# Row transfers, GpSimd gates and elementwise sums of tiles in a two-layer attention kernel

## The chip, the cores and the metric

The kernel runs on one core of one Trainium2 chip. The metric is device time in microseconds (us), the median of several executions. A core has TensorE (PE: matmuls; PEld is its weight load), VectorE (DVE), ScalarE (ACT), GpSimd (POOL) and the queues that issue transfers (SP, and ACT's own). Each engine takes its instructions in the order of the program; engines wait for each other by semaphores.

## The reference

Two layers over 1024 latent tokens and 256 context tokens, width 1024, all in fp32. Layer 0 has two attentions side by side, 8 heads each, in groups of four heads that share keys and values; layer 1 has a convolution and a neighbourhood attention. What matters here is the softmax of layer 0:

```python
def gqa_attend(q, k, v, bias=None, sink=None):
    s = jnp.einsum("bqhgd,bkhd->bhgqk", q, k) * ATTN_SCALE
    if bias is not None:
        s = s + bias
    if sink is not None:        # windowed attention: one learned logit per head
        p = jax.nn.softmax(jnp.concatenate([s, sink_col], axis=-1), axis=-1)[..., :-1]
    else:
        p = jax.nn.softmax(s, axis=-1)
    return jnp.einsum("bhgqk,bkhd->bqhgd", p, v)

y_lat = jnp.concatenate([oa * jax.nn.silu(ag), ob * jax.nn.silu(bg)], axis=-1) @ w_out
```

The global attention (oa) sees all 1280 tokens. The windowed one (ob) sees the context and its own block of 128 tokens with one neighbour on each side, and has the sink. Each output is multiplied by a gate before the out-projection.

## The kernel before

**Precision.** An fp32 product is made of three matmuls in TensorE's fast format: each operand is split into a high part (a cast on ScalarE) and a low part (a subtraction on GpSimd or VectorE, `split`).

**Units and groups.** Layer 0's attention has four units of four heads: 2 and 3 are windowed, 0 and 1 global; they run in the order 2, 3, 0, 1. A unit has ten groups, one for each block of 128 queries (QORD: blocks 2, 3, 4, 0, 5, 6, 1, 7, 8, 9); a group's tile of queries is 512 columns wide, four heads by 128. Blocks 0 and 1 are context and have two tiles of keys. The other groups have ten in a global unit, and five (four at the edges) in a windowed one. Layer 1 has 16 groups of seven tiles.

**One tile** (`attn_gen`): two score matmuls into a bank st (L529 with QH, the high and low keys stacked; L533 with QL), in some windowed tiles a mask matmul, an exponential to pf, a split into ph and pl, and three tiles later (LOOK0) three value matmuls into a bank ov (L480 to L482). The value tile V has 64 columns of low parts, 64 of high parts and 64 of ones, so that L480 and L482 also sum the denominators into rows 64 to 127 of ov. There are two st banks, one ov bank and two mx banks.

**Group change.** `attn_prep` finds the maxima of the group after next: score estimates in a bank mx, reduced on VectorE (L645, L656, L664). For windowed groups VectorE then takes the maximum with the sink, and with ScalarE makes the sink's own term (L439 to L446). `attn_fin` transposes the result on TensorE (L457) and VectorE spreads it over four heads into rows 64 and up of QL (L458), which enter the score through the ones in KB. After the last tile a windowed group adds its sink with one more matmul (L485). VectorE then transposes, inverts and transposes back the denominators, multiplies ov by them (L693) and by the gate gt (L695).

**Filler.** `weave` lets projections (pq, pg), their tails (trk) and the modulation weights (`mod_steps`: pm, two loads of 1 MB ahead of each half) run between the steps of attention. A scheduler orders all of it on each engine by priority and by its own estimate of when operands are ready; the filler has the lower priority.

Of the kernel before, what the change touches and what calls it, by code (L numbers as in the profile page):

```python
# [10 lines left out]
F32 = mybir.dt.float32  # L11
# [7 lines left out]
P = 128  # L19
# [14 lines left out]
LOOK0, LOOK1 = 3, 3  # L34
AHEAD = 3
# [54 lines left out]
def tile_kernel(ctx: ExitStack, tc: tile.TileContext, a, out):  # L90
# [11 lines left out]
    mk, mwp, layer = [0], [None], [0]  # L102
# [112 lines left out]
    def mod_steps(pool, halves):  # L215

        def load(l, part, j):
            ws = []
            for d in (0, 4):
                w = pool.tile([P, 4, 512], F32, tag="mw", name=nm("mw"), bufs=2)  # L220
                SY.dma_start(w, mod_src(l, part, j, d, d + 4))
                ws.append(w)
            return ws

        ws = load(*halves[0])
        for n_, hf in enumerate(halves):
# [4 lines left out]
            for d, w in enumerate(ws):  # L231
                mod_part(pb, w, range(4 * d, 4 * d + 4))
# [5 lines left out]
            if n_ + 1 < len(halves):  # L238
                ws = load(*halves[n_ + 1])
# [153 lines left out]
    bd = const("k_bd", [12, 4], SC)  # L393
# [29 lines left out]
    def attn_prep(pool, g):  # L423
# [8 lines left out]
        yield from g.maxes(QH, mp)  # L432
        nr = 12 if g.sink is not None else 4
        nmt = pool.tile([P, 12], F32R, tag="nmt", name=nm("nmt"), bufs=2)
        if g.sink is None:
            VE.tensor_reduce(nmt[:, 0:4], mp[:, :, 0 : g.nmp], axis=AX.X, op=ALU.max)
        else:
            m8 = pool.tile([P, 4], F32, tag="m8", name=nm("m8"), bufs=2)
            VE.tensor_reduce(m8, mp[:, :, 0 : g.nmp], axis=AX.X, op=ALU.max)  # L439
            sk1, sk8 = g.sink  # L440
            VE.tensor_tensor(nmt[:, 0:4], m8, sk8, op=ALU.max)
            se = pool.tile([P, 4], F32, tag="se", name=nm("se"), bufs=2)
            VE.scalar_tensor_tensor(se, nmt[:, 0:4].bitcast(F32), -SCALE, sk1, op0=ALU.mult, op1=ALU.add)
            SC.activation(se, se, AF.Exp)
            VE.tensor_copy(nmt[:, 4:8], se)
            VE.tensor_tensor(nmt[:, 8:12], se, nmt[:, 4:8].bitcast(F32), op=ALU.subtract)  # L446
# [3 lines left out]
    def attn_fin(g):  # L450

        nr, nmt, QL = g.nr, g.nmt, g.QL
        for _ in range(FIN[layer[0]]):
            yield
        tr2 = bank("mx", nm("trn"))
        with tc.issue_after(sts[-1].ins) if sts else ExitStack():
            PE.transpose(tr2[0:nr, 0:P], nmt[:, 0:nr].bitcast(F32), ident)  # L457
        VE.tensor_tensor(QL[64 : 64 + nr, :].rearrange("p (h q) -> p h q", h=4),  # L458
# [4 lines left out]
    def attn_gen(pool, groups, vshare, look, nexts=None):  # L463
# [6 lines left out]
        def flush():  # L470
# [12 lines left out]
            if last:  # L483
                if g.sink is not None:
                    PE.matmul(g.ov, g.skm(), g.QL[0:76, :], start=False, stop=True)  # L485
# [17 lines left out]
        for _ in attn_fin(groups[0]):  # L503
            pass
# [1230 lines left out]
```

## Time and profile before

| | us |
|---|---|
| three runs | 1528.69, 1532.21, 1532.37 |
| median | 1532.21 |
| span of the profiled execution | 1528.5 |
| mean granted clock of TensorE | 0.976 |

Layer 0's attention lies between about 146 and 905 us of the span, the convolution between 940 and 1110, layer 1's attention from 1199 on. In the profile's rows a tile is named without its number; `pl<-pf,ph` is an instruction that writes pl and reads pf and ph; x is a count. A releaser is what ended an engine's idle time. Durations of matmuls overlap, so their pitch has to be read from start to start.

### The profile page before, as it was taken

The page shows a single profiled execution, that of the slowest core. Times are in us where ns is not written, and L with a number is a line of the kernel's source. Part 1 is how long each engine was busy: PE and PEld are TensorE (multiplying, and loading weights), DVE is VectorE, ACT ScalarE, POOL GpSimd, SP SyncE. Part 2 cuts the span into 40 slices and gives each one's busy share as a digit, 9 for nine tenths or more (in the row PEclk, how much of TensorE's full clock was granted, in tenths as well). Part 3 has the DMA queues.
Part 4 walks back from the last instruction along what each step waited for, and adds up shares of the span by engine and source line. Part 5 has one row for each costly group of instructions (what it writes and reads, how often), then busy time and mean ns, then how long its engine had stood idle before and what let it go on. Part 6 is the DMA issues. An engine that isn't in the chain of part 4 may idle for free.

```text
span 1528.5 us, 21545 instructions
## 1 busy us (share of the span) xinstructions
PE 1451.0 (95%) x7144; PEld 1167.2 (76%) x7144; DVE 1031.7 (67%) x2095; ACT 748.1 (49%) x1418; POOL 788.0 (52%) x628
## 2 busy tenths in 40 slices
PE   6999999998998999999999889999999999989996
PEld 2786877896896777886777568888887788868775
DVE  2643566589578856457676948899848666567766
ACT  3642433443435564447646665343334455455564
POOL 3360443555454766557645665665532434364665
PEclk9999999999999999999999999999999999989998
DMA  9564325422312246121202021210484677877642
GB/s 366 201 225 135 106 69 174 135 77 88 114 56 76 85 138 210 49 69 54 59 28 66 35 67 56 62 56 28 158 253 144 207 219 240 248 222 234 178 129 110
DMA packets 154167, 199.83 MB, mean 131 GB/s; under 512 B 14716, under 2 KB 95816, under 8 KB 154056
## 3 DMA queue, kind: packets, MB, share of 16 engines
q1 hardware_dynamic: 147392, 186.88, 38.9%
q10 hardware_dynamic: 6664, 11.57, 2.3%
q8 instruction: 56, 0.92, 0.3%
q14 instruction: 55, 0.45, 0.1%
HBM read 148.07 MB, written 49.02 MB: 129 GB/s over the span
## 4 chain that ended last, share of the span: by engine, by line
PE 79%; DVE 11%; issue 3%; DMA 3%; ACT 2%; POOL 1%; ACTq 0%; SPq 0%; DVEq 0%; POOLq 0%
PE p L352 6%; PE p L354 6%; PE p L353 6%; PE ov L480 5%; PE ov L482 4%; PE ov L481 4%; PE po L352 4%; PE st L533 4%; PE st L529 4%; PE po L353 4%; PE po L354 4%; PE pq L352 4%; PE pq L353 3%; PE pq L354 3%; PE pg L352 2%
## 5 line engine op out<-in xcount | busy, mean ns | idle before, releaser
L334 POOL TENSOR_TENSOR pl<-pf,ph 128x512 fp32r<-128x512 f32 (+4 forms) x321 | 394.0, 1239 | 384.9 <-ACT ph L331 337.3
L541 ACT ACTIVATE pf<-st 128x512 f32<-128x512 f32 x284 | 166.5, 597 | 203.6 <-PE st L533 165.2
L334 POOL TENSOR_TENSOR wl<-wr,wh 128x512 fp32r<-128x512 f32 (+2 forms) x131 | 169.3, 1302 | 136.5 <-ACT wh L331 124.0
L331 ACT CAST ph<-pf 128x512 fp32r<-128x512 f32 (+4 forms) x364 | 209.5, 588 | 27.1 <-PE ov L481 15.9
L352 PE MATMUL p<-hh,wh 128*128 128x512 f32 x448 | 176.0, 393 | 3.4 <-DVE spq L1233 1.3
L353 PE MATMUL p<-hl,wh 128*128 128x512 f32 x448 | 174.5, 390 | 0.0
L354 PE MATMUL p<-hh,wl 128*128 128x512 f32 x448 | 173.0, 391 | 0.0
L480 PE MATMUL ov<-ph,Vt 128*128 128x512 f32 (+4 forms) x364 | 141.0, 387 | 4.2 <-DVE y L693 2.0
L529 PE MATMUL st<-QH,KAt 128*128 128x512 f32 (+4 forms) x364 | 140.2, 386 | 3.9 <-ACT pf L541 3.1
L482 PE MATMUL ov<-pl,Vt 128*128 128x512 f32 (+4 forms) x364 | 141.1, 388 | 2.2 <-POOL pl L334 2.1
L481 PE MATMUL ov<-ph,Vt 128*64 128x512 f32 (+4 forms) x364 | 138.9, 381 | 0.0
L533 PE MATMUL st<-QL,KBt 68*128 68x512 f32 (+4 forms) x364 | 136.4, 386 | 0.9 <-issue 0.8
L1177 DVE SCALAR_TENSOR_TENSOR cps<-U,taps,cps 128x512 f32<-128x512 f32 x184 | 125.9, 748 | 0.7
L331 ACT CAST wh<-wr 128x512 fp32r<-128x512 f32 (+2 forms) x134 | 80.9, 613 | 84.1 <-PE po L353 15.9
L352 PEld LDWEIGHTS p<-hh,wh 128*128 128x128 f32 x448 | 84.2, 188 | 21.5 <-ACT spq L1231 1.6
L656 DVE TENSOR_REDUCE mp<-mx 128x1 f32<-128x512 f32 x128 | 85.3, 681 | 19.3 <-PE mx L655 18.3
L354 PEld LDWEIGHTS p<-hh,wl 128*128 128x128 f32 x448 | 84.1, 188 | 17.4
L353 PEld LDWEIGHTS p<-hl,wh 128*128 128x128 f32 x448 | 84.2, 188 | 17.1 <-issue 0.2
L1020 DVE SCALAR_TENSOR_TENSOR x<-po,modT,x 128x512 f32<-128x512 f32 (+1 forms) x72 | 46.9, 657 | 64.0 <-PE po L354 63.5
L352 PE MATMUL pq<-wh,hh 128*128 128x384 f32 x256 | 88.2, 344 | 1.0 <-ACT hh L331 1.0
L353 PE MATMUL pq<-wl,hh 128*128 128x384 f32 x256 | 87.3, 341 | 0.0
L354 PE MATMUL pq<-wh,hl 128*128 128x384 f32 x256 | 86.6, 342 | 0.0
(287 smaller groups left out, 3417.2 us busy)
## 6 DMA issues: line engine op xcount, KB each, us to landing
mw<-in_mod_w_dram SPq DMA_DIRECT2D x16, 1024.0 KB, 5.3
Q<-qs SPq DMA_DIRECT2D x40, 256.0 KB, 2.1
QH<-Q SPq DMA_DIRECT2D x80, 128.0 KB, 2.7
mw<-in_mod_w_dram SPq DMA_DIRECT2D x16, 512.0 KB, 6.8
wr<-in_od_d_dram SPq DMA_DIRECT2D x32, 256.0 KB, 3.1
wr<-in_ev_qkv_dram SPq DMA_DIRECT2D x16, 384.0 KB, 5.0
KAt<-KD SPq DMA_DIRECT2D x16, 384.0 KB, 6.5
wr<-in_od_wo_dram SPq DMA_DIRECT2D x22, 256.0 KB, 3.4
```

The lines of the kernel that those rows point to most:

```text
L331: acts.append(SC.copy(hi, src))
L334: (GP if leng == "g" else VE).tensor_tensor(lo, src, hi.bitcast(F32), op=ALU.subtract)
L352: PE.matmul(o, lh, rh, start=first, stop=False)
L353: PE.matmul(o, lh, rl, start=False, stop=False)
L354: last.append(PE.matmul(o, ll, rh, start=False, stop=end))
L480: PE.matmul(o, V[:, 64:192], ph[:, :n], start=(t == 0), stop=False)
L481: PE.matmul(g.ov[0:64, q0 : q0 + n], V[:, 0:64], ph[:, :n], start=False, stop=False)
L482: PE.matmul(o, V[:, 64:192], pl[:, :n], start=False, stop=(last and g.sink is None))
L529: sts.append(PE.matmul(st[:, :n], KA[:, cs], g.QH[:, q0 : q0 + n], start=True, stop=False))
L533: PE.matmul(st[:, :n], KB[0:68, cs], g.QL[0:68, q0 : q0 + n], start=False, stop=True)
L541: acts.append(SC.activation(pf[:, :n], st[:, :n], AF.Exp, scale=1.0 if g.bias else SCALE))
L1177: VE.scalar_tensor_tensor(pc, uc, w, pc, op0=ALU.mult, op1=ALU.add)
```

## The change

1. **Maxima by transfer.** KB has one row of -1 in place of four of ones. `attn_fin` copies the transposed maxima (4 rows, or 12 with the sink) to SBUF on ScalarE, and a transfer on ScalarE's queue lays them out as one row (or three) of QL. The broadcast on VectorE is gone, in both layers.
2. **Gate on GpSimd.** In layer 0 the inverse denominators are multiplied by the gate on GpSimd before they meet ov. The factor 0.5 goes into V's ones, now 2.
3. **Sink elsewhere.** The sink's logit is copied by ScalarE into the maxima before they are reduced; its term is made in `attn_fin` by GpSimd and ScalarE.
4. **Sums over tiles.** In units 2 and 3, for blocks 2 and up, the exponentials of all tiles are added up elementwise in a tile acc: three of the four additions on GpSimd, the last (every fourth) on VectorE. ADV and UADD set this. A value tile then takes two matmuls in place of three. At the end acc is split, and two matmuls with ones and the sink's one make the denominators in a bank dn; ov's halves are added after a copy on ScalarE.
5. **Buffers.** The modulation weights come in loads of 512 KB with three buffers in place of 1 MB with two: a half's fourth load takes the buffer of its first. The squares at the end of layer 0 have fewer buffers of their own.

The core of the diff:

```diff
         def load(n):
+            l, part, j = halves[n // 4]
+            w = pool.tile([P, 2, 512], F32, tag="mw", name=nm("mw"), bufs=3)
+            SY.dma_start(w, mod_src(l, part, j, 2 * (n % 4), 2 * (n % 4) + 2))
...
-            for d, w in enumerate(ws):
-                mod_part(pb, w, range(4 * d, 4 * d + 4))
+            for d in range(4):
+                mod_part(pb, ws.pop(0), (2 * d, 2 * d + 1))
+                if 4 * n_ + d + 3 < 4 * len(halves):
+                    load(4 * n_ + d + 3)
...
-        GP.memset(KB[64:68, :].bitcast(F32), 1.0)
+        GP.memset(KB[64:65, :].bitcast(F32), -1.0)
...
+        if g.sink is not None:
+            SC.copy(mp[:, :, g.nmp], g.sink[1])
+        yield from g.maxes(QH, mp)
+        VE.tensor_reduce(nmt[:, 0:4], mp[:, :, 0 : g.nmp + (g.sink is not None)], axis=AX.X, op=ALU.max)
...
+    def attn_fin(pool, g):
+        if g.sink is not None:
+            GP.tensor_tensor(se, g.sink[1], nmt[:, 0:4].bitcast(F32), op=ALU.subtract)
+            yield
+            SC.activation(se, se, AF.Exp, scale=SCALE)
+            SC.copy(nmt[:, 4:8], se)
+            yield
+            GP.tensor_tensor(nmt[:, 8:12], se, nmt[:, 4:8].bitcast(F32), op=ALU.subtract)
...
-        VE.tensor_tensor(QL[64 : 64 + nr, :].rearrange("p (h q) -> p h q", h=4),
-                         tr2[0:nr, None, 0:P].broadcast_to([nr, 4, P]),
-                         bd[0:nr, :, None].broadcast_to([nr, 4, P]), op=ALU.mult)
+        nq = QL[96 : 96 + nr, 0:P]
+        SC.copy(nq, tr2[0:nr, 0:P])
+        (SC, SY)[QDE].dma_start(QL[64 : 64 + nr // 4, :].bitcast(F32).rearrange("j (h q) -> j h q", h=4),
+                                                          nq.bitcast(F32))
...
+            if g.adds:
+                both = [(o, V[:, 0:128], ph), (o[0:64], V[:, 64:128], pl)]
+                for x_, v_, p_ in both[::-1] if last else both:
+                    PE.matmul(x_, v_, p_[:, :n], start=(t == 0 and p_ is ph), stop=(last and p_ is ph))
...
+            if g.adds:
+                dn = bank("tr", nm("dn"))
+                for k_, x in enumerate(g.acs):
+                    PE.matmul(dn[0:64, :], ones64[0] if layer[0] else V[:, 128:192], x, start=(k_ == 0), stop=(k_ == 1 and g.sink is None))
...
+            if g.adds and t > 0:
+                a_ = g.acc[:, q0 : q0 + n]
+                (VE if (t + ADV[layer[0]]) % 4 == 0 else GP).tensor_tensor(a_, a_, pf[:, :n], op=ALU.add)
+            if g.adds and t == len(g.tiles) - 1:
+                g.acs = [pool.tile([P, 512], F32R, tag=x, name=nm("ac" + x), bufs=look + 1) for x in ("ph", "pl")]
+                split(g.acc, *g.acs, "s", "v")
...
+    def ADDS(u, qb):
+        return qb >= 2 and u in UADD
...
+            if g.adds:
+                for es, cs in half:
+                    acts.append(SC.copy(y2[es], ov[64:128, cs]))
+                for es, cs in half:
+                    VE.tensor_tensor(y2[es], ov[0:64, cs], y2[es], op=ALU.add)
...
+            GP.tensor_tensor(rb, rb, g.gt.rearrange("p a q -> p (a q)"), op=ALU.mult)
-            VE.scalar_tensor_tensor(y, y, 0.5, g.gt, op0=ALU.mult, op1=ALU.mult)
```

**TensorE at the first group change of unit 3.** Before (trn is the transpose of the maxima, mx the estimates for a later group, pq a projection):

```order
L457 MATMUL trn_2811<-ident,nmt_2767 12x128
L643 MATMUL mx_2832<-KAt_489,QH_2817 128x256 x2
L352 MATMUL pq_3728<-wh_3068,hh_174 128x384
L353 MATMUL pq_3728<-wl_3069,hh_174 128x384
L354 MATMUL pq_3728<-wh_3068,hl_175 128x384
```

Now, at the same change:

```order
L461 MATMUL trn_2897<-ident,nmt_2794 12x128
L666 MATMUL mx_2919<-KAt_488,QH_2901 128x256 x2
L188 MATMUL pm_3241<-mw_2075,csil 32x512 x2
L188 MATMUL pm_3241<-mw_2079,csil 32x512 x2
L188 MATMUL pm_3241<-mw_2083,csil 32x512 x2
L666 MATMUL mx_2925<-KAt_488,QH_2901 128x256 x2
L686 MATMUL mx_2929<-KAt_488,QH_2901 128x384
L544 MATMUL st_2995<-QL_2777,KBt_483 128x512
L544 MATMUL st_3020<-QL_2777,KBt_483 128x512
```

The score matmuls with QL stand seven rows behind the transpose, and no projection stands between them; three pieces of a modulation half do, and its fourth follows seven rows later. The projections of this place stand earlier and later in the order.

**ScalarE at the next group change of unit 3, now** (the ACTIVATE rows are exponentials of a score bank; y is the copy of ov's upper half):

```order
L334 CAST ph_3221<-pf_3223 128x512
L452 CAST nmt_2917<-se_3004 128x4
L718 COPY y_3384<-ov_3260 64x256 x2
L463 CAST QL_2902<-trn_3011 12x128
L334 CAST acph_3228<-acc_3000 128x512
L464 DMA QL_2902<-QL_2902 3x4x128
L555 ACTIVATE acc_3268<-st_3263 128x512
```

Of these rows only the first and the last kind stood on ScalarE before. The row's copy and its transfer stand behind the copies of ov, which need the last value matmul, and the transfer also behind the cast of the summed tile.

**GpSimd over the first of these groups.** Before (pl is the low part of a tile of exponentials, wl that of a weight, pc and Vt the projection's tails):

```order
L334 TENSOR_TENSOR pl_2911<-pf_2912,ph_2910 128x512
L249 TENSOR_TENSOR nr_3828<-ss_3825,mhalf 128x10
L334 TENSOR_TENSOR pl_2931<-pf_2932,ph_2930 128x512
L334 TENSOR_TENSOR pl_3048<-pf_3049,ph_3047 128x512
L334 TENSOR_TENSOR wl_4017<-wr_4015,wh_4016 128x512
L334 TENSOR_TENSOR pl_3129<-pf_3130,ph_3128 128x512
```

Now:

```order
L337 TENSOR_TENSOR pl_2999<-acc_3000,ph_2998 128x512
L337 TENSOR_TENSOR pl_3024<-pf_3025,ph_3023 128x512
L561 TENSOR_TENSOR acc_3000<-acc_3000,pf_3025 128x512
L449 TENSOR_TENSOR se_3004<-sink_160,nmt_2917 128x4
L337 TENSOR_TENSOR pl_3140<-pf_3141,ph_3139 128x512
L252 TENSOR_TENSOR nr_3357<-ss_3354,mhalf 128x10
L561 TENSOR_TENSOR acc_3000<-acc_3000,pf_3141 128x512
L252 TENSOR_TENSOR nr_3517<-ss_3514,mhalf 128x10
L337 TENSOR_TENSOR pl_3222<-pf_3223,ph_3221 128x512
L454 TENSOR_TENSOR nmt_2917<-se_3004,nmt_2917 128x4
L561 TENSOR_TENSOR acc_3000<-acc_3000,pf_3223 128x512
```

Between the splits now stand the additions into acc, two powers of the projection's norms and the sink's subtractions.

Over the whole program TensorE has 76 value matmuls fewer and 32 for denominators more; VectorE has 56 broadcasts, 40 gate products and 80 small operations of the sink fewer, and 12 additions, 16 splits and 32 halves' additions more; GpSimd has 48 additions, 40 gate products and 40 small operations more; ScalarE has 56 row copies with their transfers, 16 casts of acc, 32 copies of ov's halves and 40 small copies more.

More of the change, by code (lines that the diff above doesn't have):

```diff
@@ L215, in mod_steps, with load @@
     def mod_steps(pool, halves):
[L217 to L225, printed above, removed]
+        def load(n):
+            l, part, j = halves[n // 4]
+            w = pool.tile([P, 2, 512], F32, tag="mw", name=nm("mw"), bufs=3)
+            SY.dma_start(w, mod_src(l, part, j, 2 * (n % 4), 2 * (n % 4) + 2))
+            ws.append(w)
+        ws = []
+        for n in range(3):
+            load(n)
         for n_, hf in enumerate(halves):
@@ L390, in silu2 @@
         VE.scalar_tensor_tensor(dst, dst, 1.0, psrc, op0=ALU.add, op1=ALU.mult)
-    bd = const("k_bd", [12, 4], SC)
+    cp.tile([P, 8], F32, tag="cpad", name="cpad")
     Ks, Vs = [], []
@@ L431, in attn_prep @@
         mp = pool.tile([P, 4, 4], F32, tag="mp", name=nm("mp"), bufs=2)
-        yield from g.maxes(QH, mp)
         nr = 12 if g.sink is not None else 4
         nmt = pool.tile([P, 12], F32R, tag="nmt", name=nm("nmt"), bufs=2)
[L435 to L446, printed above, removed]
+        if g.sink is not None:
+            SC.copy(mp[:, :, g.nmp], g.sink[1])
+        yield from g.maxes(QH, mp)
+        VE.tensor_reduce(nmt[:, 0:4], mp[:, :, 0 : g.nmp + (g.sink is not None)], axis=AX.X, op=ALU.max)
         g.nmt, g.nr = nmt, nr
         yield
-    def attn_fin(g):
+    def attn_fin(pool, g):
         nr, nmt, QL = g.nr, g.nmt, g.QL
-        for _ in range(FIN[layer[0]]):
+        if g.sink is not None:
+            se = pool.tile([P, 4], F32, tag="se", name=nm("se"), bufs=2)
+            GP.tensor_tensor(se, g.sink[1], nmt[:, 0:4].bitcast(F32), op=ALU.subtract)
             yield
+            SC.activation(se, se, AF.Exp, scale=SCALE)
[3 more added lines that the diff above has]
+            yield
+        else:
+            for _ in range(FIN[layer[0]]):
+                yield
         tr2 = bank("mx", nm("trn"))
@@ L502, in attn_gen @@
                     yield
-        for _ in attn_fin(groups[0]):
+        for _ in attn_fin(kvs[-1], groups[0]):
             pass
@@ L1061, in final_proj @@
                     if c < 2:
[L1062 removed]
+                        sq = op_.tile([P, 512], F32, tag="sq1", name=nm("sq1"), bufs=2)
                     else:
@@ L1434, in finish @@
                     split(y[ds], od3[hf][ds, 0], od3[hf][ds, 1], "s", "v")
-            g = Group(no=gi, copy=lambda: copy_k(hd), load_q=load_q, load_b=load_b, maxes=maxes, nmp=2, bias=True, ahead=ahead, sink=None, tiles=tiles, den=den, finish=finish,
+            g = Group(no=gi, copy=lambda: copy_k(hd), load_q=load_q, load_b=load_b, maxes=maxes, nmp=2, bias=True, ahead=ahead, sink=None, tiles=tiles, finish=finish, adds=False,
                       start=start, gate=gate,
```

104 lines of the change are left out of this document (58 added, 46 removed).

## The prediction

> **What bounds the kernel now.** I read the page first, then the busy times of chosen stretches, TensorE's own waits, the timeline for the pitch of its matmuls, and the groups of instructions for durations.
>
> ```profile
> span 1528.5 us, 21545 instructions
> PE 1451.0 (95%) x7144; PEld 1167.2 (76%) x7144; DVE 1031.7 (67%) x2095; ACT 748.1 (49%) x1418; POOL 788.0 (52%) x628
> PE 79%; DVE 11%; issue 3%; DMA 3%; ACT 2%; POOL 1%; ACTq 0%; SPq 0%; DVEq 0%; POOLq 0%
> ```
>
> TensorE is busy for 95% of the span and makes 79% of the chain that ended last. So a change pays in two ways only: fewer passes on TensorE, or fewer of the 77.5 us in which it stands still (1528.5 - 1451.0). No other engine is near its limit over the whole span; in single stretches some are.
>
> ```profile
> core 0: us, PE busy (x) PEld busy (x) DVE busy (x) ACT busy (x) POOL busy (x), PEclk, DMA share, GB/s
> 330.00:360.00 30.00, 27.82 (x160) 23.36 (x159) 27.97 (x53) 12.67 (x28) 17.42 (x14) 1.00 0.31 98
> 360.00:380.00 20.00, 18.09 (x76) 13.80 (x76) 17.81 (x40) 10.26 (x23) 11.48 (x8) 0.85 0.24 79
> 460.00:520.00 60.00, 53.14 (x269) 42.21 (x267) 53.90 (x116) 29.75 (x64) 33.09 (x26) 0.97 0.26 81
> PE mx L655 <- DVE mp L656: 7.8, 14, 1.9
> PE trn L457 <- DVE nmt L436: 2.5, 3, 1.0
> PE trn L457 <- DVE nmt L446: 2.1, 3, 1.3
> PE ov L482 <- POOL pl L334: 2.1, 4, 1.2
> PE mx L643 <- DVE QL L458: 1.8, 3, 1.1
> ```
>
> The first stretch and the second hold the first groups of unit 3. VectorE is busy for 45.8 of 50 us there, TensorE for 45.9, and after 4.1 us of its idleness the granted clock falls to 0.85. In 460 to 520, where windowed groups give way to global ones without filler, TensorE misses 6.9 us and VectorE is busy for 53.9 of 60. The waits (total, times, longest) name VectorE 14.2 us in these four rows and GpSimd 2.1. So VectorE does end the waits in layer 0. GpSimd is today hardly waited for.
>
> **The change, term by term.** The sum is made against the profiled span, 1528.5 us. The three runs have their median at 1532.2, 3.7 us above it; I add these at the end.
>
> *Matmuls.* 76 score tiles (two windowed units, eight groups of 4 or 5 tiles) lose one of three value passes, and 16 groups gain two passes over the summed tile: 44 passes fewer. What one is worth is its pitch, not its duration.
>
> ```profile
> 301.59 0.39 PE L480 MATMUL ov<-ph,Vt 128*128 128x512 f32 x1
> 301.82 0.40 PE L481 MATMUL ov<-ph,Vt 128*64 128x512 f32 x1
> 302.06 0.33 PE L352 MATMUL pq<-wh,hh 128*128 128x384 f32 x1
> 302.23 0.34 PE L353 MATMUL pq<-wl,hh 128*128 128x384 f32 x1
> 211.48 1.00 PE pm L185 x8
> 212.85 0.97 PE pm L185 x2
> ```
>
> A pass of 512 columns starts 0.234 us after the last (301.59 to 302.06 for two), with 64 columns of weights as with 128. So 44 x 0.234 = **-10.3 us**, not 44 x 0.39. A modulation piece costs some 0.95 us of TensorE whether four of its instructions run beside each other (1.00) or one alone (0.97; the profile shows each as two). The order has 28 such pieces before and 26 after: **-2**.
>
> *GpSimd.* It gains 48 additions of 128x512, 40 products of 128x256 and 40 tiny operations, and loses none. Their nearest rows, with those of the operations around them:
>
> ```profile
> L334 POOL TENSOR_TENSOR pl<-pf,ph 128x512 fp32r<-128x512 f32 x270 | 352.7, 1318 | 325.1 <-ACT ph L331 290.6 <-PE ov L481 6.5 <-PE ov L482 6.1
> L1067 POOL TENSOR_TENSOR acc<-acc,sq 128x512 f32<-128x512 f32 x2 | 3.1, 1528 | 1.0 <-ACT sq L1065 1.0
> L334 POOL TENSOR_TENSOR wl<-wr,wh 128x256 fp32r<-128x256 f32 x20 | 15.0, 763 | 3.9 <-ACT wh L331 3.8
> L249 POOL TENSOR_TENSOR nr<-ss,mhalf 128x10 f32<-128x10 f32 x10 | 19.6, 1963 | 17.9 <-DVE ss L907 8.8 <-PE mx L643 6.4 <-PE ov L482 2.5
> L924 POOL TENSOR_TENSOR pc<-pc,rt 128x640 f32<-128x640 f32 x16 | 25.9, 1620 | 20.3 <-DVE pc L922 15.4 <-DVE m L439 2.4 <-DVE ss L907 0.8
> L331 ACT CAST ph<-pf 128x512 fp32r<-128x512 f32 x300 | 182.4, 622 | 20.0 <-PE ov L481 11.0 <-DMA x<-in_xT_dram 2.7 <-PE p L354 1.1
> L541 ACT ACTIVATE pf<-st 128x512 f32<-128x512 f32 x284 | 166.5, 597 | 203.6 <-PE st L533 165.2 <-POOL pl L334 24.6 <-DVE pl L334 6.2
> L331 ACT CAST qs<-trk 128x256 fp32r<-128x256 f32 x40 | 15.0, 374 | 31.7 <-PE trk L932 29.7 <-issue 1.3
> L331 ACT CAST KAt<-trk 64x128 fp32r<-64x128 f32 x40 | 10.3, 258 | 30.2 <-DVE qs L334 30.2
> ```
>
> At 1.32 to 1.53 us an addition, 48 of them are 63 to 73 us, and the products 40 x 0.76 = 31. Beside projection work this lies under TensorE's passes (GpSimd is busy for 52%). It doesn't where filler is missing, and the order shows such a place: between the transposes that open unit 3's first group and its third, TensorE had 117 projection passes before and has **none** after. What is left there for TensorE is 45 passes of 512 columns (10.5 us), eight each of 384 and 256 (8 x 0.17 + 8 x 0.12 = 2.3), three modulation pieces (2.9) and under 1 of small ones: 16.6 us. GpSimd has, from the first split of that stretch to the operation that frees the third transpose, eight splits and six additions (14 x 1.32 = 18.5), three powers (5.9), one rotation (1.6), one product (0.8) and four tiny ones (0.8 at 0.2 each, taken from VectorE's 0.16 for such a tile, below): 27.6 us. TensorE needs these splits, so it stands at least 27.6 - 16.6 = 11 us.
>
> GpSimd can't run through either. At a group change the new tile of queries waits for: two value passes and the transpose (0.7), two copies on ScalarE (2 x 0.37), its copy of the row (0.26), the cast of the summed tile that stands ahead of the transfer (0.62), issue and landing of the transfer, two score passes (0.5), two exponentials and a cast (1.8). For issue and landing the nearest rows are these.
>
> ```profile
> L1007 ACTq DMA_DIRECT2D x<-in_xT_dram x8: 374/422/528, 571.2 to 582.9; - x8
> L613 SPq DMA_DIRECT2D KBt<-KAt x8: 498/531/571, 94.3 to 719.7; - x8
> DMA to landing us min/median/max: 2.2/2.6/3.1
> Od<-y SPq DMA_DIRECT2D x30, 128.0 KB, 1.8
> QL<-QD SPq DMA_DIRECT2D x16, 128.0 KB, 4.6
> ```
>
> From 1.8 (a store in a quiet stage) to 4.6 us (layer 1); I take 2.6, the one copy within SBUF, and 0.4 to issue. The chain is 7.6 us; GpSimd has about 3 us left to do meanwhile, so it starves some 4.5 us at each of two changes: up to 20 us of idle TensorE. Between 11 and 20 I take 16. The 4.1 us that it stands there today go: **+12**. The clock falls there now and will then: 0 (up to +3 for a second fall; 0.15 x 20 in the row above).
>
> *VectorE.* It loses the broadcast of the maxima (682 ns, 56 times), the gate's product and the sink's operations, and gains two adds, a split and a quarter of the accumulations in the 16 groups.
>
> ```profile
> L458 DVE TENSOR_TENSOR QL<-trn,k_bd 4x512 fp32r<-4x512 f32 x36 | 24.6, 682 | 22.1 <-PE trn L457 21.2
> L695 DVE SCALAR_TENSOR_TENSOR y<-y,gt 128x256 f32<-128x256 f32 x40 | 25.6, 639 | 0.8
> L441 DVE TENSOR_TENSOR nmt<-m,sink x20: 148/163/1277, 133.4 to 481.0; 128x4 fp32r<-128x4 f32 x20
> ```
>
> That is 1.3 us for each of 20 groups of the global units, 0.7 for each of layer 1's 16. The most that it can give is the 14.2 us of waits above; those on the running maxima (mx) need the whole queue to be shorter. I take **-5**, bounds 0 and -14.
>
> The last row shows a tile of four columns at a median of 163 ns and once at 1277, about one GpSimd pass. The Trainium skill says in "SBUF — State Buffer", section "Who interferes with whom", that a VectorE instruction with two inputs in SBUF and a GpSimd instruction that reads SBUF exclude each other for a whole instruction. By that rule each of the 88 large operations moved to GpSimd can hold VectorE up for its length, and in the stretch above, where both would be full, 16 us would become some 20 and the time 1542; the row agrees with it, but shows no total, and I leave it out of the sum.
>
> *Rows by transfer elsewhere.* The broadcast was 0.68 us on VectorE; now copy, issue and landing take 3.3. In most groups the order leaves 4 to 30 us of passes between transpose and use, which hide it. It leaves under 2 us at unit 0's first group, unit 1's fifth group and layer 1's first group; queued behind the waiting score pass are all later passes. At 1.5, 1.5 and (with 4.6 to land) 3 us less what hides: **+4**, bounds 0 and 8.
>
> *Modulation weights.* In each of eight halves the fourth load of 512 KB starts only when the first piece has been used. In four halves just 1.2 to 3.1 us of passes lie between that piece and the fourth.
>
> ```profile
> mw<-in_mod_w_dram SPq DMA_DIRECT2D x16, 1024.0 KB, 5.3
> hl<-Od SPq DMA_DIRECT2D x6, 512.0 KB, 4.8
> ```
>
> 1024 KB landed in 5.3, 512 KB of another tensor in 4.8. With 4 to 5 us, one of the four hidden in the stretch above: **+4**, bounds 0 and 9.
>
> *Other windowed groups.* One more run of some 16 us of passes without filler appears in unit 3, with GpSimd about as loaded: **+3**, bounds 0 and 6. ScalarE's extra copies, casts and issues (56 x 0.7, 16 x 0.6, 32 x 0.37) lie on an engine that is busy for 49%; fewer buffers for the squares at the end of layer 0, other constants: 0, at most 1 if those squares wait.
>
> Sum: -10.3 - 2 + 12 - 5 + 4 + 4 + 3 = +5.7, so 1534.2 on the profiled scale and **1538** for the median.
>
> **Rivals.** (a) *GpSimd keeps up*: other work fills unit 3's first groups or splits run ahead, and TensorE stands no longer than its 4 us there. Then the sum is -10.3 - 2 - 5 + 4 = -13, **1519**. It needs GpSimd's 27.6 us to fit TensorE's 16.6, so splits and additions under about 0.5 us, or a backlog worked off beforehand. For it: GpSimd is idle half the time and waited for only 2.1 us. Against: those rows were paid with filler beside them. (b) *The stretch costs only GpSimd's excess*, 11 - 4 = 7 us, and transfers and loads hide: -10.3 - 2 + 7 - 5 + 4 + 3 = -3, **1529**, no measurable change. (c) *The new chain decides everywhere*: ScalarE, in order, stands behind the copies that await the last value pass, so each of 16 groups starts 1 to 1.5 us late even beside filler, +20 on the sum: **1557**. The distances of 5 us and more speak against it.
>
> **How the numbers follow.** Forecast 0.40 (1533 to 1548), (a) 0.29, (b) 0.21, (c) 0.10. A measurement tells 0.3% or 4.6 us from no change: faster is below 1527.6, slower above 1536.8. Of the forecast's own 0.40 some 0.06 lies within 0.3%, and of (b) 0.02 below. So faster is 0.29 + 0.02 = 0.31, same 0.19 + 0.06 = 0.25, slower 0.34 + 0.10 = 0.44. All terms at their low ends give -20 (1512), at their high ends +32 (1564); leaving a tenth out on either side, 1515 to 1556.
>
> **What would show it.** In the changed profile, unit 3's first three groups with TensorE idle for over 10 us, waiting on GpSimd's pl or on QL's transfer, show the main step right; a busy TensorE there shows it wrong. TensorE's total of value passes must fall by 76 and rise by 32. Waits of pm on mw tell the loads; score passes (L544) that wait for a DMA tell the row; rows of mx on mp under 7.8 us tell VectorE's relief. It would be wrong above all if the stretch's missing filler costs nothing, or if layer 1 reacts by more than 3 us.

## The result, and the profile after

The changed kernel is slower: 1593.79 us, median of four runs (1591.4 to 1596.21), against 1530.45 before, a ratio of 1.040 (95% interval 1.0373 to 1.0426). Some 58 of the 63 us were not forecast. The page of the changed kernel, its lines on the span and the busy times of the engines, and its chain of waits by engine:

```profile
span 1589.6 us, 21810 instructions
PE 1478.0 (93%) x7100; PEld 1173.6 (74%) x7100; DVE 1008.4 (63%) x1963; ACT 791.9 (50%) x1562; POOL 891.7 (56%) x756
PE 72%; DVE 11%; DMA 5%; POOL 4%; issue 4%; ACT 2%; SPq 1%; ACTq 0%; POOLq 0%; DVEq 0%
```

TensorE has 44 matmuls fewer (7100 for 7144), as counted, and yet is busy for 27 us more. Busy time of TensorE is stretched by its clock (the value passes at 339.95 and 345.71 in the rows below, before and after the clock fell, take 0.39 and 0.69 us), and the mean granted clock fell from 0.976 to 0.951. It stands still for 111.6 us (1589.6 - 1478.0) in place of 77.5. VectorE lost 23 us of work, GpSimd gained 104.

The next two answers give the busy times in two stretches of unit 3: from the transpose that opens its first group to the one that opens its fourth, and on to the end of the unit. First the kernel before, then the changed one (length, then busy us and instructions of PE, PEld, DVE, ACT, POOL, then the granted clock):

```profile
330.50:387.10 56.60, 52.51 (x261) 42.38 (x260) 48.21 (x99) 25.38 (x56) 30.77 (x22) 0.94 0.28 89
387.10:499.80 112.70, 108.43 (x550) 92.07 (x549) 85.15 (x203) 48.28 (x98) 55.85 (x42) 0.98 0.26 79
```

```profile
328.60:383.90 55.30, 39.34 (x126) 25.46 (x127) 39.51 (x82) 24.32 (x57) 37.69 (x35) 0.63 0.27 84
383.90:530.00 146.10, 131.94 (x630) 105.63 (x627) 101.58 (x197) 63.92 (x143) 93.38 (x81) 0.93 0.26 80
```

The unit takes 201.4 us in place of 169.3. In its first three groups TensorE now stands for 16.0 us (55.30 - 39.34) where it stood for 4.1, at a clock of 0.63. Those groups are no longer than before; but 126 matmuls ran in them in place of 261. The missing ones are projections, and they are made up later: the rest of the unit has 80 matmuls more and takes 33 us longer. There too TensorE stands for 14.2 us, not 4.3. GpSimd is busy for 131 us in the unit; it was 87.

The unit holds only half of the loss. The starts of the transposes divide the two profiled spans, and that of the kernel without the sums (first experiment below), like this (us):

| | to unit 2 | layer 0's attention, first to last transpose | from there to layer 1's first transpose | layer 1's attention to the end |
|---|---|---|---|---|
| before | 146.4 | 736.4 | 316.3 | 329.4 |
| changed | 147.2 | 774.5 | 333.5 | 334.4 |
| without the sums | 148.6 | 742.9 | 330.7 | 335.3 |

So 38 of the 61 us between the two spans lie in layer 0's attention and 17 between it and that of layer 1. The sums cost 32 of the former and 3 of the latter.

TensorE's waits in the first three groups after the change (who waited for whom, total, times, longest):

```profile
PE ov L488 <- DVE nt L253: 5.4, 1, 5.4
PE dn L498 <- ACT acph L334: 2.8, 1, 2.8
PE st L540 <- ACT pf L555: 1.9, 1, 1.9
PE trn L461 <- POOL nmt L454: 1.3, 1, 1.3
PE ov L488 <- POOL pl L337: 1.3, 1, 1.3
PE st L544 <- DMA QL<-QL: 1.1, 1, 1.1
```

(Five rows of 1.1 us and less are left out.) The longest names VectorE. The value pass that waits reads a tile pl, though, and pl comes from GpSimd. The timeline of that place, GpSimd's rows, then TensorE's, then two of VectorE's (start, duration, engine, instruction; in brackets the idle time before it):

```profile
337.82 1.27 POOL L337 TENSOR_TENSOR pl<-pf,ph 128x512 fp32r<-128x512 f32 x1
339.19 1.96 POOL L252 TENSOR_TENSOR nr<-ss,mhalf 128x10 f32<-128x10 f32 x1
341.13 1.26 POOL L561 TENSOR_TENSOR acc<-acc,pf 128x512 f32<-128x512 f32 x1
342.35 1.96 POOL L252 TENSOR_TENSOR nr<-ss,mhalf 128x10 f32<-128x10 f32 x1
344.28 1.38 POOL L337 TENSOR_TENSOR pl<-pf,ph 128x512 fp32r<-128x512 f32 x1
```

```profile
339.95 0.39 PE L488 MATMUL ov<-pl,Vt 128*64 128x512 f32 x1
345.71 0.69 PE L488 MATMUL ov<-pl,Vt 128*64 128x512 f32 x1 [5.37 <-DVE nt L253]
```

```profile
341.19 1.22 DVE L253 TENSOR_TENSOR nt<-nr,ss 128x10 f32<-128x10 f32 x1 [1.05 <-POOL nr L252]
344.46 1.23 DVE L253 TENSOR_TENSOR nt<-nr,ss 128x10 f32<-128x10 f32 x1
```

The split that the value pass needs stands in GpSimd's queue behind two powers of the projection's norms and one addition, 5.2 us together. It ends at 345.66, and the pass starts at 345.71. nt at 344.46 merely ends a moment later (345.69). So the engine that is named is not always the one that was waited for. With this one, 8.0 us of these waits go back to GpSimd (5.4, 1.3, 1.3), 4.7 to ScalarE and 1.1 to the row's transfer.

### The profile page after: what moved, and what is told of

The parts are those of the page before. It is cut to its first block, busy times and chain, and to the rows that moved or that the text cites. A ratio compares the mean times of both kernels' runs of the same rounds, so it can differ in the third digit from the quotient of the medians.

```text
span 1589.6 us, 21810 instructions
## 1 busy us (share of the span) xinstructions
PE 1478.0 (93%) x7100; PEld 1173.6 (74%) x7100; DVE 1008.4 (63%) x1963; ACT 791.9 (50%) x1562; POOL 891.7 (56%) x756
## 4 chain that ended last, share of the span: by engine, by line
PE 72%; DVE 11%; DMA 5%; POOL 4%; issue 4%; ACT 2%; SPq 1%; ACTq 0%; POOLq 0%; DVEq 0%
PE p L355 5%; PE p L357 5%; PE p L356 5%; PE po L355 4%; PE po L356 4%; PE po L357 4%; PE st L540 4%; PE st L544 4%; PE ov L490 4%; PE ov L492 4%; PE ov L491 3%; PE pg L355 2%; PE pg L356 2%; PE pg L357 2%; PE pq L357 2%
## 5 line engine op out<-in xcount | busy, mean ns | idle before, releaser
L337 POOL TENSOR_TENSOR pl<-pf,ph 128x512 fp32r<-128x512 f32 (+4 forms) x305 | 376.0, 1241 | 250.9 <-ACT ph L334 194.4
L555 ACT ACTIVATE pf<-st 128x512 f32<-128x512 f32 x268 | 158.3, 596 | 139.9 <-PE st L544 83.6
L334 ACT CAST ph<-pf 128x512 fp32r<-128x512 f32 (+4 forms) x348 | 201.4, 586 | 36.9 <-PE ov L491 11.3
L540 PE MATMUL st<-QH,KAt 128*128 128x512 f32 (+4 forms) x364 | 146.9, 405 | 11.4 <-ACT pf L555 7.6
L544 PE MATMUL st<-QL,KBt 65*128 65x512 f32 (+4 forms) x364 | 140.5, 399 | 2.3 <-DMA QL<-QL 2.3
L490 PE MATMUL ov<-ph,Vt 128*128 128x512 f32 (+4 forms) x288 | 112.5, 391 | 2.7 <-DVE y L730 1.9
L492 PE MATMUL ov<-pl,Vt 128*128 128x512 f32 (+4 forms) x288 | 112.1, 389 | 2.5 <-POOL pl L337 2.5
L491 PE MATMUL ov<-ph,Vt 128*64 128x512 f32 (+4 forms) x288 | 110.6, 384 | 0.0
L540 PEld LDWEIGHTS st<-QH,KAt 128*128 128x128 f32 x364 | 71.3, 196 | 38.4 <-ACT pf L555 18.0
L668 DVE TENSOR_REDUCE mp<-mx 128x2 f32<-128x512 f32 x80 | 54.5, 685 | 62.2 <-PE mx L666 61.7
```

What stands on the lines that cost most here:

```text
L334: acts.append(SC.copy(hi, src))
L337: (GP if leng == "g" else VE).tensor_tensor(lo, src, hi.bitcast(F32), op=ALU.subtract)
L490: PE.matmul(o, V[:, 64:192], ph[:, :n], start=(t == 0), stop=False)
L491: PE.matmul(o[0:64], V[:, 0:64], ph[:, :n], start=False, stop=False)
L492: PE.matmul(o, V[:, 64:192], pl[:, :n], start=False, stop=(last and g.sink is None))
L540: sts.append(PE.matmul(st[:, :n], KA[:, cs], g.QH[:, q0 : q0 + n], start=True, stop=False))
```

## The experiments

Three theories stood at first. A: GpSimd's additions starve TensorE in unit 3. B: the sums leave TensorE too little to do there, and any engine would be late. C: the other parts cost the time. Later ones are stated where they come up. Each median is compared with that of the kernel before measured beside it; these lay between 1530.25 and 1532.28. Where two experiments are compared that were not measured together, the accuracy is those 2 us.

**The sums and who adds.** Four kernels: `UADD = ()`; all additions on VectorE; `UADD = (2,)`; and the sink's two subtractions on VectorE.

```diff
-UADD = (2, 3)
+UADD = ()
```

> The changed kernel without part 4: no tile is summed elementwise, every tile has its three value passes again; row transfers, gate on GpSimd, sink operations and loads stay. Theory A (GpSimd's additions, in order between the splits, starve TensorE where no filler stands, and the clock halves after it): unit 3 loses its 40 us of extra idleness and half clock, the passes come back with 10: about 1555, and 1545 if what was lost after unit 3 was its echo. Theory B (the sums only shorten TensorE's work and so use up the filler; any engine would be late): the same, 1545 to 1555. Theory C (row transfers, gate, sink and loads cost the time by themselves): 1580 or more, with TensorE idle for 10 us or more in unit 3's first three groups.

Measured: 1559.65, ratio 1.0176 (1.0146 to 1.0206). The sums cost 34 us, and 27 are left without them; A and B had both forecast some 5 us less. Unit 3's first three groups, but for their last 1.6 us (the fourth transpose starts at 384.55):

```profile
325.80:383.00 57.20, 56.24 (x303) 46.83 (x302) 41.88 (x87) 26.19 (x65) 34.01 (x31) 1.00 0.28 91
```

To that transpose they take 58.8 us with 310 matmuls, 3.5 us more than with 126. TensorE stands for 1.0 us and its clock stays full. So the sums empty this stretch of projections without making it longer. C explains 27 us at most; A and B are both left standing.

```diff
-(VE if (t + ADV[layer[0]]) % 4 == 0 else GP).tensor_tensor(a_, a_, pf[:, :n], op=ALU.add)
+VE.tensor_tensor(a_, a_, pf[:, :n], op=ALU.add)
```

> The changed kernel with all 64 additions on VectorE, none on GpSimd; the order of TensorE still has no projection in unit 3's first groups. Theory A: GpSimd keeps up, TensorE's idleness in unit 3 falls from 30 us to 15 or less, the half clock with it: 1550 to 1565. Theory B: TensorE still stands about as long: 1585 to 1600. Theory C: no change, 1590.

Measured: 1600.5, ratio 1.0452 (1.042 to 1.0484). Theory A, that GpSimd's additions are the cause, falls. The first three groups and the rest of unit 3:

```profile
329.30:379.10 49.80, 37.75 (x130) 22.88 (x131) 46.33 (x93) 25.34 (x57) 36.72 (x30) 0.81 0.29 93
379.10:528.70 149.60, 133.78 (x647) 108.12 (x646) 113.56 (x225) 64.66 (x150) 77.24 (x68) 0.93 0.26 80
```

The groups are 5 us shorter, with VectorE busy for 46 of 50; the rest is 3 us longer. The unit takes 199.4 us, not 201.4: VectorE's queue has taken the place of GpSimd's. TensorE's largest waits in the groups now name ScalarE's exponentials (6.1 us), and the largest waits of those name VectorE's additions (5.7 us).

```diff
-UADD = (2, 3)
+UADD = (2,)
```

> The changed kernel with the sums in unit 2 alone, where projections stand beside every group. Theory A: unit 3 runs about as before the change, unit 2 keeps its 5 us of saved passes: 1545 to 1555. Theory B: the filler runs out earlier by those 5 us only: 1550 to 1560. Theory C: 1585 or more.

Measured: 1574.13, ratio 1.0275 (1.0242 to 1.0308). That is 14 us over the kernel without sums, though unit 2 has 38 value passes fewer and only 16 for denominators more. The forecasts of A and of B were both too low. Unit 3, which sums nothing here, again has no projections in its first group; its first three groups take 66.2 us with 249 matmuls.

```diff
-            GP.tensor_tensor(se, g.sink[1], nmt[:, 0:4].bitcast(F32), op=ALU.subtract)
+            VE.tensor_tensor(se, g.sink[1], nmt[:, 0:4].bitcast(F32), op=ALU.subtract)
...
-            GP.tensor_tensor(nmt[:, 8:12], se, nmt[:, 4:8].bitcast(F32), op=ALU.subtract)
+            VE.tensor_tensor(nmt[:, 8:12], se, nmt[:, 4:8].bitcast(F32), op=ALU.subtract)
```

> The changed kernel with the two tiny subtractions of the sink's term on VectorE in place of GpSimd, so that the transpose of the maxima no longer waits for GpSimd's queue. Theory A: the splits still wait for GpSimd; only the waits of the transpose go (2.9 us): 1585 to 1592. Theory C in its form 'tiny operations queued on GpSimd decide at the group changes': 1570 or less.

Measured: 1580.04, ratio 1.0307 (1.0267 to 1.0346), 14 us under the changed kernel and between the two forecasts, for 40 operations that kept GpSimd busy for 11.3 us in all. The waits that the profile names for them are 2.9 us. The rest is what stands behind such an operation in an ordered queue, or the order of the projections, which moved with it; this run does not tell the two apart. How far it moved, the units show: unit 3 now takes 179.1 us in place of 201.4, but unit 0 takes 248.5 in place of 227.9. So the length of one unit is no price; only that of all together is.

**One unit, and the other parts.** Here theory D was stated: projections are used up in unit 2.

```diff
-UADD = (2, 3)
+UADD = (3,)
```

> The changed kernel with the sums in unit 3 alone. Theory D (new, since the additions on VectorE gained nothing and the sums in unit 2 alone still cost unit 3 its time: unit 2's saved passes are filled with projections of unit 0, which then stop, because their keys and values go into the buffers that unit 2 still reads; unit 3's first groups have no filler): unit 2 uses no more projections than without the sums, unit 3 keeps some at its start, 1555 to 1568. Theory B' (unit 3's own shorter tiles and the longer chain at its group changes cost the time): 1575 to 1590.

Measured: 1591.75, ratio 1.0408 (1.0385 to 1.0431). Theory D falls as it was put: sums in unit 3 alone cost 32 us over none, almost what sums in both do. The order again has no projections at unit 3's second and third group, though unit 2 saves nothing. B', that unit 3's own tiles cost it, gave 1575 to 1590, so it was just missed. The first three groups and the rest of unit 3:

```profile
324.10:368.10 44.00, 37.44 (x162) 30.33 (x161) 31.23 (x62) 19.14 (x45) 28.23 (x28) 0.85 0.11 31
368.10:518.00 149.90, 136.58 (x661) 110.97 (x659) 102.30 (x208) 68.78 (x158) 101.36 (x88) 0.93 0.27 85
```

With the same sums these groups, of which the first still has projections, are 11 us shorter than in the changed kernel, and the time of the whole is the same. Their length alone does not decide the loss.

The next three leave the sums out and undo one more part each: the gate's product on VectorE behind the product with ov; the spread of the maxima on VectorE into four rows; loads of 1 MB and the squares' buffers as before.

```diff
-            GP.tensor_tensor(rb, rb, g.gt.rearrange("p a q -> p (a q)"), op=ALU.mult)
...
+            VE.tensor_tensor(y, y, g.gt, op=ALU.mult)
```

> The changed kernel without the sums (1560) and with the gate's product back on VectorE, behind ov times the inverse denominators. If the hop to GpSimd at each group's end, with a single ov bank, makes the other 27 us: 1540 to 1548, above all in unit 1's last groups and at the end of layer 0. If not: 1556 to 1562.

```diff
-        SC.copy(nq, tr2[0:nr, 0:P])
-        (SC, SY)[QDE].dma_start(...)
+        VE.tensor_tensor(QL[64 : 64 + nr, :].rearrange("p (h q) -> p h q", h=4), ..., op=ALU.mult)
```

> The changed kernel without the sums and with the maxima spread by VectorE into four rows of QL, as before, in both layers; no row transfer. If the transfer's 3 us at groups without filler make the other 27 us: 1540 to 1550, with gains at the first group of each layer. If it relieved VectorE by more than it delays: 1562 to 1570.

```diff
-            w = pool.tile([P, 2, 512], F32, tag="mw", name=nm("mw"), bufs=3)
+                w = pool.tile([P, 4, 512], F32, tag="mw", name=nm("mw"), bufs=2)
...
-            pool, tag, bufs = (kvp, "QH", 3) if c == 2 else (a0, "acc", 2)
+            pool, tag, bufs = (kvp, "QH", 3) if c == 2 else (op_, "acc1", 1)
```

> The changed kernel without the sums and without part 5: two loads of 1 MB ahead of each half of the modulation weights, and the buffers of the squares as before. If the fourth load's waits and the pieces that no longer run beside each other make the other 27 us: 1545 to 1552, and 9 us less at least in the waits of pm. If not: 1557 to 1562.

Measured: 1557.91 (gate, ratio 1.0182, 1.0164 to 1.0201), 1560.09 (row, 1.0199, 1.0175 to 1.0224) and 1566.99 (loads and buffers, 1.0241, 1.0222 to 1.0261), against 1559.65. Gate and row transfer, undone singly, give back nothing beyond the 2 us of accuracy. The third is even slower. The traces show what hides behind these totals. Without row transfers layer 1's attention to the end takes 327.8 us, not 335.3, but layer 0's attention 751.3, not 742.9. With the old loads and buffers the stretch between the two layers takes 325.6 us, not 330.7, but layer 0's attention 755.1, not 742.9. That projections moved by undoing a part make this loss in layer 0 was not shown; the parts were therefore tried alone.

**What a pass is worth, and the parts alone.** One more score pass ahead of each summed tile's own:

```diff
+            if g.adds:
+                PE.matmul(st[:, :n], KA[:, cs], g.QH[:, q0 : q0 + n], start=True, stop=True)
```

> The changed kernel with one more score pass for every summed tile (QH against the same keys, into the bank that the real pass then overwrites): 76 passes or 17.8 us of TensorE more than the changed kernel, more than the sums save. Theory P (in units 2 and 3 TensorE does not set the pace; what the sums save there only goes into idle time, where the clock halves): 1585 to 1598, no clear difference from 1594, and idleness of TensorE in unit 3 some 5 us or more lower. Rival (TensorE's passes set the pace, and the loss comes from the longer work at the group changes): 1604 to 1612.

Measured: 1606.77, ratio 1.0479 (1.0442 to 1.0515): 13 us more for 17.8 us of passes. Theory P falls for the two units as wholes: a pass costs most of its price there, as if TensorE set the pace beside projections. This is one run, and the order moved with it.

The sums alone (with part 5, whose memory they need): gate and row undone by the edits above, and the sink back on VectorE by this one.

```diff
-            SC.copy(mp[:, :, g.nmp], g.sink[1])
...
+            VE.tensor_tensor(nmt[:, 0:4], m8, sk8, op=ALU.max)
+            VE.scalar_tensor_tensor(se, nmt[:, 0:4].bitcast(F32), -SCALE, sk1, op0=ALU.mult, op1=ALU.add)
+            SC.activation(se, se, AF.Exp)
+            VE.tensor_copy(nmt[:, 4:8], se)
+            VE.tensor_tensor(nmt[:, 8:12], se, nmt[:, 4:8].bitcast(F32), op=ALU.subtract)
```

> The changed kernel with parts 1, 2 and 3 undone: maxima spread by VectorE, gate's product on VectorE, sink as before; the sums and the smaller loads stay. Theory P: the sums cost unit 3 its time by themselves: 1560 to 1575. Rival (the loss in unit 3 needs the row transfers and the hops to GpSimd at the group changes as well): 1530 to 1545.

Measured: 1573.32, ratio 1.0266 (1.0228 to 1.0304). This lies in the range that theory P gave. Against part 5 alone (1543.5, below) the sums cost 30 us. They need neither row transfers nor hops to GpSimd. In 32 us of unit 3's second and third group:

```profile
338.00:370.00 32.00, 20.66 (x62) 13.56 (x62) 31.07 (x60) 12.62 (x26) 21.80 (x15) 0.68 0.18 53
```

Here VectorE, which keeps the broadcast, the gate and the sink, is busy for 31.07 us and has no room left.

No sums, and the sink back by the same edit (`UADD = ()`):

> The changed kernel without the sums (1560) and with the sink's maximum and term on VectorE as before. If the sink's tiny operations, queued on GpSimd and ScalarE, make the 27 us that are left without the sums: 1540 to 1548. If those come from parts 1, 2 and 5: 1556 to 1562.

No sums, with gate, row, loads and squares undone by the edits shown, so that part 3 stands alone:

> Part 3 alone: the changed kernel without the sums and with row transfers, gate and loads undone, so that only the sink's operations stand elsewhere than before. If parts 1, 2 and 5 make the 27 us by adding up (5 in layer 1, 4 in unit 1, 14 in the first group, the out-projection and the convolution's start): 1530 to 1537. If part 3 does: 1545 or more.

Measured: 1549.82 (ratio 1.0106, 1.0063 to 1.0149) and 1544.81 (1.0079, 1.0049 to 1.0108). The sink's part costs 10 us by the first and 13 by the second. The expectation that parts 1, 2 and 5 make all of the 27 was wrong. The cost lies in layer 0's attention (742.9 us without the sums, 733.9 once the sink is back as well; 736.4 before, 746.9 with part 3 alone), but in no one place there; unit 1, which has no sink, shares in it. What passes it on was not found.

**What was still open.** Eight more score passes ahead of each of the 14 tiles of unit 3's first three groups (`warm`):

```diff
+            for _ in range(8 if g.warm else 0):
+                PE.matmul(st[:, :n], KA[:, cs], g.QH[:, q0 : q0 + n], start=True, stop=True)
```

> The changed kernel with eight more score passes ahead of each tile of unit 3's first three groups (14 tiles, 112 passes, 26 us of TensorE at full clock), overwritten by the real ones. Theory W (16 us of idleness there cost another 14 by the halved clock, and the saved passes had no other place to go): the passes fill the idleness and keep the clock up, half-clock loss there 4 us or less, 1585 to 1600. Rival (the halved clock only goes with the waits and costs little by itself): 1608 to 1620.

Measured: 1594.14, ratio 1.0414 (1.0379 to 1.045): 26 us of passes cost nothing in the total, as theory W has it. The three groups:

```profile
329.70:387.40 57.70, 50.06 (x208) 34.99 (x206) 40.14 (x82) 24.51 (x58) 39.52 (x34) 0.91 0.24 76
```

TensorE stands for 7.6 us, the clock is 0.91, and yet the groups are 2 us longer. So it is open whether the clock's loss was the price or only a mark of waiting.

Part 5 alone (parts 1 to 3 undone by the edits above, `UADD = ()`):

> The changed kernel with parts 1 to 4 undone: only the loads of 512 KB with three buffers and the squares' fewer buffers stay. If these make about half of the 27 us that are left without the sums (first group, out-projection, start of the convolution): 1540 to 1548. If they are free and the rest is parts 1 to 3: 1529 to 1535.

Measured: 1543.5, ratio 1.0079 (1.0052 to 1.0107): part 5 costs 12 us, when the forecast had 4 to 5.

On that kernel, sums in the global unit 0, every other addition on VectorE:

```diff
-UADD = ()
+UADD = (0,)
...
-(VE if (t + ADV[layer[0]]) % 4 == 0 else GP).tensor_tensor(a_, a_, pf[:, :n], op=ALU.add)
+(VE if t % 2 else GP).tensor_tensor(a_, a_, pf[:, :n], op=ALU.add)
```

> The kernel of the run before with sums in the global unit 0, whose tiles of ten per group save 64 passes (15 us); every other addition on VectorE. Theory V (a summed tile saves 0.23 us of TensorE and asks 0.7 to 1.3 us of VectorE or GpSimd, and pays only beside projections; without them the adders set the pace): 5 to 25 us slower than the run before, with idle TensorE in unit 0's groups without projections. Rival (only the windowed units, short of projections, make the sums dear): 8 to 15 us faster than the run before.

Measured: 1579.04, ratio 1.032 (1.0279 to 1.036), 35 us over part 5 alone; the direction of theory V, and more than it said. In unit 0 without projections:

```profile
496.20:561.00 64.80, 51.78 (x167) 32.73 (x167) 53.15 (x81) 36.97 (x67) 51.07 (x38) 0.83 0.11 36
```

VectorE and GpSimd are each busy for some 80%, and TensorE stands for 13 us. The sums are dear in another unit too.

Three added passes in place of eight:

```diff
-            for _ in range(8 if g.warm else 0):
+            for _ in range(3 if g.warm else 0):
```

> As the run with eight added score passes ahead of each tile of unit 3's first three groups (1594, no dearer than the changed kernel), but three: 42 passes, 10 us. If the halved clock itself sets the pace there, the added passes keep it up at less than they cost: 1575 to 1588, and the three groups shorter than the 55 us of the changed kernel by 6 us or more. If VectorE, GpSimd and ScalarE with the waits between them set the pace (theory O), passes and clock are both free there: 1588 to 1599, the three groups 52 to 58 us long.

Measured: 1607.71, ratio 1.0481 (1.0444 to 1.0519). The time fits neither theory. The three groups do:

```profile
330.30:388.10 57.80, 44.86 (x163) 30.29 (x164) 40.74 (x82) 24.39 (x56) 38.55 (x35) 0.76 0.25 80
```

They take 57.8 us, as theory O has it. The profiled execution is 18.9 us longer than that of the changed kernel: 2.5 in these groups, 5.9 in the rest of the unit, 8.8 behind it and 1.7 ahead. The order of the later groups differs; nothing here tells why they take longer. So a change that moves the order can shift 10 us and more elsewhere, and a single total tells the price of a part no finer than that.

The small loads alone: part 5 alone with the squares' buffers as before.

```diff
-            pool, tag, bufs = (kvp, "QH", 3) if c == 2 else (a0, "acc", 2)
+            pool, tag, bufs = (kvp, "QH", 3) if c == 2 else (op_, "acc1", 1)
...
-                        sq = op_.tile([P, 512], F32, tag="sq1", name=nm("sq1"), bufs=2)
+                        sq = op_.tile([P, 512], F32, tag="sq1", name=nm("sq1"), bufs=3)
```

> The kernel with part 5 alone (1543), but with the squares' buffers at the end of layer 0 as before: of the change only the modulation loads of 512 KB with three buffers are left. The loss of part 5 alone lies behind unit 1, from the out-projection to the convolution's start, while the modulation loads end at 422 us: if it is the squares' buffers, 1529 to 1535; if the loads cost it by a later effect, 1540 to 1546.

Measured: 1535.78, ratio 1.0027 (1.0008 to 1.0047). The small loads cost 4 us, the squares' buffers the other 8. In all runs the stretch from layer 0's last transpose to layer 1's first agrees: it takes 316.2 to 325.6 us in the four kernels with the old buffers for the squares, 329.2 to 335.0 in the fifteen with the new ones. The first and last pass of layer 1's projection p, before, with part 5 alone, and with the small loads alone:

```profile
L352 PE MATMUL p<-hh,wh x448: 387/389/798, 929.4 to 1326.0; 128*128 128x512 f32 x150
```

```profile
L355 PE MATMUL p<-hh,wh x448: 387/389/798, 938.7 to 1342.7; 128*128 128x512 f32 x150
```

```profile
L355 PE MATMUL p<-hh,wh x448: 387/389/793, 937.8 to 1334.0; 128*128 128x512 f32 x150
```

From first to last it takes 396.6, 404.0 and 396.2 us, so the squares' 8 us lie in there. The squares feed the normalisation ahead of p; that this is the way by which they delay it was not shown.

## Why the prediction was wrong, point by point

The sign was right, the size was not: 1538 was forecast, and 1594 lies beyond the range's end of 1556 and beyond every rival; the last, (c), had 1557.

The step that failed is the price of the sums. The forecast saved their passes at full pitch and charged only the idle time of TensorE that it saw in the order: -10.3 + 12 + 3 = +4.7. The runs show 30 us for the sums alone and 34 beside the other parts. Two terms put at a gain or at nothing make most of the rest: the sink's part and the squares' buffers.

Measured alone or one upon the other, the parts come to the whole: small loads 4, squares' buffers 8 (1543.5 - 1535.78), sink 13, row and gate 6 (1549.82 - 1543.5), sums 30, together 61 of 63. This holds for one order of adding them. Without part 5, parts 1 to 3 cost 37 (1566.99 - 1530.25), and part 5 then gives 7 back.

- *Matmuls, -10.3.* The count is right: 76 value passes fewer, 32 for denominators more. The worth is not. Over the two units a pass was worth some 0.7 of its pitch by one run (13 of 17.8 us); in unit 3's first groups it is worth little (26 us of passes made them 2.4 us longer).
- *The stretch at unit 3's first groups, +12.* The place and the idleness are as forecast: 16 was said, and TensorE stands for 14.6 us from the first transpose to the third, 16.0 in the three groups, against 4.1. GpSimd's work is right too (28.2 us busy for 27.6). That the sum fits is partly luck: the chain of the row's copy and transfer was to give up to 9 us, and the waits name the transfer for 1.1. What failed is to take idle time for the whole price. The stretch was put at 16.6 us of work for TensorE plus 16 of waits; from the first transpose to the third it took 42.2 us (328.6 to 370.8), 25.6 over the work. The clock, put at 0 to +3, was 0.64, and the work itself took 27.6. And the missing projections have to run somewhere else.
- *What sets the length of these groups.* The changed kernel and the two with added passes put 126, 163 and 208 matmuls into them, at clocks of 0.63, 0.76 and 0.91, and take 55.3, 57.8 and 57.7 us. Neither passes nor clock set the length there. That the other engines do, with the waits between them, is the likely reading, but it was argued and not shown: in the changed kernel VectorE and GpSimd are busy for 71% and 68% of it, in fixed queues, and with the additions on VectorE that engine had 93%. Against a single limit speak the 44.0 us with the sums in unit 3 alone. That GpSimd's 27.6 us would decide was at most half of it, therefore.
- *Other windowed groups, +3.* This term was far too small. In the rest of unit 3 TensorE stands for 14.2 us against 4.3, and the clock is 0.93 against 0.98. Of 131.94 busy us 0.07 is 9, of 108.43 us 0.02 is 2. So +17, by an estimate that counts the clock's loss in full.
- *VectorE relief, -5.* It failed, and its sign with it. The waits of mx on mp, its sign, stood at 7.8 us in their largest row and now at 6.9, but all such rows of layer 0 come to 13.5 us, and were 11.4. VectorE lost 23 us of work, but a part that was to relieve it, the sink's, cost 10 to 13. The prediction priced its tiny operations by their duration; two in each group, moved, gave back 14 us.
- *The rule weighed there.* The Trainium skill's "SBUF — State Buffer", section "Who interferes with whom", lets a VectorE instruction with two inputs in SBUF wait for a whole GpSimd instruction that reads SBUF. The trace agrees: the 128x10 product of nt takes 1202 ns in the median after the change and 172 before (rows below), and the one at 341.19 ends at 342.41, with GpSimd's addition (342.39). By that rule 1542 was given, and the time lies far beyond it; it bears on the size of VectorE's relief, and no run here tells how many us it makes in all.
- *Row transfers, +4; loads, +4.* Row and gate together cost 6, undone singly nothing; the prediction's +4 is within what these totals can tell. It had called itself wrong if layer 1 reacted by more than 3 us, and it does: from its first transpose to the end it takes 5.0 us more than before. The seven kernels without row transfers have 323.7 to 332.6 us there, the twelve with them 333.6 to 338.9. The loads cost 3.7 (1535.78 against 1532.06). The -2 for the modulation pieces came: their matmuls are busy for 42.0 us, and were for 43.8.
- *Squares' buffers, 0 to 1.* They cost 8, behind layer 0's attention; the forecast had put them at next to nothing without a row to go by.

The product of nt before and after (duration ns min, median, max):

```profile
L250 DVE TENSOR_TENSOR nt<-nr,ss x10: 159/172/1258, 298.4 to 513.9; 128x10 f32<-128x10 f32 x10
```

```profile
L253 DVE TENSOR_TENSOR nt<-nr,ss x10: 170/1202/1252, 341.2 to 572.3; 128x10 f32<-128x10 f32 x10
```

Why the projections are missing there stays open. In the order eight of unit 0's ten projection blocks stand before unit 3's first transposes, and the ninth only behind its third; unit 0's keys and values go into the buffers that unit 2 reads to its end. That this holds the ninth up was only argued: a third pair of buffers has no room, and it was not tried. Sums in either unit bring it about, in other groups each time.

## What to carry to other kernels

A TensorE pass saved is worth its pitch only where TensorE sets the pace; ask of each stretch what its length would be without filler, and price a change there by the engines that take the work over. Here a summed tile saved 0.23 us of TensorE and asked 1.29 us of GpSimd or 0.69 of VectorE. Where a scheduler places filler, read from the new order where it is now missing: a stretch that loses it costs the work that must run elsewhere, not only the idle time. Since filler moves between units, compare whole stages before a unit is blamed. Tiny operations aren't priced by their duration alone.

## What the runs showed of the hardware

In this trace TensorE's clock fell where TensorE stood, and stayed low for longer than it stood. Busy times of the changed kernel in stretches of 10 us (the columns as above):

```profile
330.00:340.00 10.00, 7.20 (x33) 3.56 (x27) 6.00 (x16) 6.20 (x13) 6.72 (x7) 1.00 0.83 257
340.00:350.00 10.00, 3.42 (x10) 1.75 (x8) 8.64 (x14) 1.92 (x6) 7.05 (x6) 0.53 0.02 7
350.00:360.00 10.00, 8.95 (x25) 6.91 (x26) 8.00 (x20) 5.27 (x9) 7.83 (x6) 0.50 0.06 13
360.00:370.00 10.00, 5.87 (x14) 3.12 (x13) 8.01 (x14) 2.33 (x6) 6.48 (x7) 0.50 0.17 52
370.00:381.00 11.00, 9.61 (x27) 6.67 (x26) 6.50 (x16) 7.15 (x21) 6.71 (x8) 0.50 0.27 86
381.00:390.00 9.00, 9.00 (x51) 8.51 (x50) 5.96 (x7) 3.12 (x6) 9.00 (x8) 0.97 0.11 32
```

The clock is halved from 340 on. Though TensorE is busy for 8.95 of the next 10 us, and without a pause from 352.6 to 363.3, it stays halved to 381, when the projections come back. What it needs to recover is not shown. Before the change it fell in these groups too, but for less: 0.85 over 360 to 380. Yet the three groups were no shorter at 0.91 than at 0.63: a low clock in the profile is a sign of waiting, and need not be its price.
